# The output gate moved from the weights of a 1024x1024 projection to the product in PSUM, by column halves

## The chip, the cores and the metric

The kernel runs on one core of one Trainium2 chip. The metric is device time in microseconds, and the time of before is 2444.82 us, the median of three runs from 2443.37 to 2444.92 us.

The engines are written as in the profile. PE is the matrix engine, and PEld is its weight load. DVE is the vector engine, ACT the scalar engine and POOL the third elementwise engine. SP is the queue from which DMA transfers are issued. SBUF is the memory that the engines work in, PSUM the memory that PE writes its products to, and DRAM the memory outside the core.

## The reference

One layer of a transformer-like block runs over 2048 tokens of 1024 channels, in fp32. What the change touches is the line in the middle:

```python
ada = jnp.einsum('bd,lde->lbe', jax.nn.silu(c), w_ada) + b_ada
sh1, sc1, g1, sh2, sc2, g2 = (m[:, None, :] for m in jnp.split(ada[l], 6, axis=-1))
...
h = modulate(rmsnorm(x, norm_mix[l]), sh1, sc1)
o, _, _ = token_mixers(h @ w_in[l], lb_f, lb_b, first, hf_c, hb_c, *mix_args)
x = x + g1 * (o @ w_out[l])
h2 = modulate(rmsnorm(x, norm_ffn[l]), sh2, sc2)
x = x + g2 * conv_ffn(h2, w_up[l], conv_w[l], conv_b[l], w_down[l], rows)
...
return rmsnorm(x, norm_final)
```

`g1` is one row of 1024 numbers that comes from the conditioning vector `c`. It multiplies the columns of the product `o @ w_out`. Multiplying the columns of `w_out` by it beforehand gives the same product.

## The kernel before, in words

**Products.** Every large product is made in three fp32r matmuls: each operand is split into a rounded high part and a low part that holds the rest, and high x high, high x low and low x high are added up in PSUM. A split is a cast on ACT (L133) and a subtraction on DVE or POOL (L134).

**Stages.** The first stage, from 0 to about 977 us, makes the input projection and the token mixers. Tasks written as Python generators run beside it: at each slot between groups of products the next piece of a task is emitted when the planner's running count of PE time has passed the number that the task yielded. One of these tasks is `w_out_ops` (L982-997). For each of 8 blocks of 128 rows and for each half of 512 columns it loads the weights, loads the gate broadcast over 128 partitions, multiplies the one by the other on DVE (L993), splits the result, and stores high and low part to the DRAM tensor `wo_d`.

**The out-projection** (the loop over 16 tiles of 128 tokens at the end of the listing) runs from about 978 to 1169 us. The mixers' output of a tile, `o`, comes from DRAM, is cast on ACT and split on DVE one tile ahead. A tile of two PSUM banks, `pd` (called `dn` in the profile, two buffers), takes the products: for each of two halves of 512 columns, eight blocks of three matmuls, so 48 matmuls a tile. Then one addition on DVE adds the residual `x` (L1358, written to `cv`), the sum is stored, and ACT squares it and sums the squares (L1360).

**The second norm.** After every second tile (an odd one) `second_norm` makes the inverse root on POOL (L126, L128), scales both tiles on DVE (L1279), and then, spread over the products of the next two tiles by the yielded waits, transposes them on PE into the PSUM tiles `ux` and `uz` (L69), applies scale and shift on ACT (L1292) and makes the combinations and splits that the next stage reads (L1295 and on). "Even transition" below is what stands between an odd tile's second half and the second half of the even tile after it; "odd transition" is the other one.

**The order.** Instructions are not issued in the order of the source: a scheduler lays each engine's list out when the kernel is built, and each engine then runs its list strictly in order, with waits on the others. The later stages are up-products with the convolution (to about 2008 us) and the down-product with the last norm.

Of the kernel before, what the change touches and what calls it, by code (L numbers as in the profile page):

```python
# [9 lines left out]
F32 = mybir.dt.float32  # L10
F32R = mybir.dt.float32r
# [7 lines left out]
P = 128  # L19
D = 1024  # L20
# [13 lines left out]
AL = 512  # L34
# [14 lines left out]
def view(t, off, dims):  # L49

    return bass.AP(t.tensor, t.offset + off, [list(t.ap[0])] + [list(d) for d in dims])
# [32 lines left out]
def tile_trunk(ctx, tc, x, c, cx, c_ctx, w_ada, b_ada, norm_mix, norm_ffn, w_in, hg_norm, sgu_g, sgu_b,  # L84
               w_sp, b_sp, w_out, w_up, conv_w, conv_b, w_down, norm_final, masks, out):
    nc = tc.nc
    V, S, G, T = nc.vector, nc.scalar, nc.gpsimd, Tensor(nc.tensor)
    ld = nc.sync.dma_start
    st = nc.sync.dma_start
# [3 lines left out]
    w_ada, w_in, w_out, w_up, w_down = w_ada[0], w_in[0], w_out[0], w_up[0], w_down[0]  # L93
# [21 lines left out]
    g_d = dr.tile([2, D], F32, name="g_d")  # L115
# [3 lines left out]
    wo_d = dr.tile([P, NK, 2, D], F32, name="wo_d")  # L119
# [3 lines left out]
    def rstd(pool, ss, n, scale, bias=EPS, keep=lambda i: i, out=None):  # L123

        r = pool.tile([P, 8], F32, tag="rs", name="rs")
        keep(G.tensor_scalar(out=r[:, :n], in0=ss, scalar1=scale, scalar2=bias, op0=ALU.mult, op1=ALU.add))  # L126
        r2 = pool.tile([P, 8], F32, tag="rs2", name="rs2") if out is None else out
        G.tensor_tensor(out=r2[:, :n], in0=r[:, :n], in1=mhalf[:, :n], op=ALU.pow)  # L128
        return r2

    def split(hi, lo, raw, eng=None, keep=lambda i: i):

        keep(S.copy(hi, raw))  # L133
        (eng or G).tensor_sub(lo, raw, hi.bitcast(F32))  # L134
# [56 lines left out]
    with es1:  # L191
# [22 lines left out]
        def raw_tile():  # L214
            return p1.tile([P, D], F32, tag="raw", name="raw", bufs=3)
# [766 lines left out]
        def w_out_ops():  # L982

            for k in range(NK):
                for n in range(2):
                    cl = slice(n * 512, n * 512 + 512)
                    raw = raw_tile()
                    w, g = raw[:, :512], raw[:, 512:]
                    ld(w, w_out[k * P:(k + 1) * P, cl])
                    ld(g, g_d[0:1, cl].broadcast_to([P, 512]))  # L990
                    yield 5.0
                    hi = pm.tile([P, 512], F32, tag="acc", name="wo_hi")
                    V.tensor_mul(w, w, g)  # L993
                    split(hi.bitcast(F32R), g.bitcast(F32R), w, V)
                    st(wo_d[:, k, 0, cl], hi)
                    st(wo_d[:, k, 1, cl], g)
                    yield 2.5

        def w_down_ops():

# [174 lines left out]
    px = esx.enter_context(tc.tile_pool(name="px", bufs=1, reuse_waits="tile"))  # L1175
# [17 lines left out]
    def dbank():  # L1193
        return ps2.tile([P, 2, 512], F32, tag="dn", name="dn", bufs=2)
# [4 lines left out]
    def v_tile():  # L1199
        return px.tile([P, TH + GW], F32, tag="cv", name="cv", bufs=3)  # L1200

    def c_tile():
        return px.tile([P, NK, P], F32R, tag="fl", name="fl", bufs=2, align_bytes=AL)
# [70 lines left out]
    with tc.tile_pool(name="po", bufs=1, reuse_waits="tile") as po:  # L1274
        def second_norm(hh, g0, xs, ss, bank_, first, step):

            r = rstd(px, ss, 2, 1.0 / D)
            for i in range(2):
                scaled.append(V.tensor_scalar(out=xs[i], in0=xs[i], scalar1=r[:, i:i + 1], scalar2=None, op0=ALU.mult))  # L1279
            yield first  # L1280
            cl = slice(g0 // 2 * P, g0 // 2 * P + P)
            for k in range(4):
                pt = bank_()
                for kk in range(2):
                    for i in range(2):
                        o = kk * 256 + i * P
                        T.transpose(pt[:, o:o + P], xs[i][:, (k + 4 * kk) * P:(k + 4 * kk + 1) * P], ident)
                yf = c_tile()
                fl = yf.bitcast(F32)
                for kk, dims in ((0, [[7 * P, 2], [1, P]]), (1, [[4 * P, 2], [1, P]])):  # L1290
                    kq = k + 4 * kk
                    pin(S.activation(view(fl, kk * P, dims),  # L1292
                                     pt[:, kk * 256:kk * 256 + 256].rearrange("p (i c) -> p i c", c=P),
                                     AF.Identity, bias=s2[:, kq:kq + 1], scale=a2[:, kq:kq + 1]))
                pin(V.tensor_sub(fl[:, 3:5, :], view(fl, 7 * P, [[-2 * P, 2], [1, P]]), view(fl, 0, [[7 * P, 2], [1, P]])))  # L1295
                V.tensor_sub(fl[:, 2, :], fl[:, 5, :], fl[:, 3, :])
                V.tensor_sub(fl[:, 6, :], fl[:, 1, :], fl[:, 2, :])
                hi = px.tile([P, 7, P], F32R, tag="yst", name="yst", bufs=2, align_bytes=AL)
                a = b = 0
                if hh == 0:  # L1300
                    a, b = NR, NR - 1
                    S.copy(xah[:, :, k, cl], fl[:, :a, :])
                    V.tensor_sub(xal[:, :, k, cl], fl[:, :b, :], xah[:, :b, k, cl].bitcast(F32))
                    V.tensor_sub(yf[:, b:a, :], fl[:, b:a, :], xah[:, b:a, k, cl].bitcast(F32))
                split(hi[:, a:, :], yf[:, a:7, :], fl[:, a:7, :], V)
                st(yd[hh][:, 0, a:, k, cl], hi[:, a:, :].bitcast(F32))
                st(yd[hh][:, 1, b:, k, cl], fl[:, b:7, :])
                yield step

        tiles = [(0, g) for g in range(NCH)] + [(1, g) for g in range(NCH)]  # L1310

        nt_ = len(tiles)

        def fetch_o(t):
            hh, g = tiles[t]
            raw = raw_tile2(2 * (t % 2 == 0)).rearrange("p a b -> p (a b)").rearrange("p (k c) -> p k c", c=P)
            ld(raw, oT_d[hh][:, :, g * P:(g + 1) * P])
            return raw

        def split_o(t, raw):  # L1320
            o = po.tile([P, 2, NK, P], F32R, tag="o", name="o", align_bytes=AL) if t % 2 else first_o[0]()
            split(o[:, 0], o[:, 1], raw, V, pin)
            return o

        def fetch_x(t):
            xt = raw_tile2(2 if t == nt_ - 1 else 1 + 2 * (t % 2))
            ld(xt.rearrange("p a b -> p (a b)"), x[t * P:(t + 1) * P, :])
            return xt.rearrange("p a b -> p (a b)")

        raw_o = {1: fetch_o(1)}  # L1330
        xts = {0: fetch_x(0)}
        ops = {0: first_o[1]}
        xs = []
        for t, (hh, g) in enumerate(tiles):
            if g % 2 == 0:
                ss = px.tile([P, 2], F32, tag="ss", name="ss", bufs=2)
            if t + 2 < nt_:
                raw_o[t + 2] = fetch_o(t + 2)
            if t + 1 < nt_:
                ops[t + 1] = split_o(t + 1, raw_o.pop(t + 1))  # L1340
                xts[t + 1] = fetch_x(t + 1)
            if t + 2 == nt_:
                units[0].load()
            if t + 1 == nt_:
                units[1].load_half(0)
            pd = dbank()
            o = ops.pop(t)
            for n in range(2):
                for k in range(NK):
                    mm3(pd[:, n, :], o[:, 0, k, :], o[:, 1, k, :], wo[k][:, 0, n * 512:(n + 1) * 512],  # L1350
                        wo[k][:, 1, n * 512:(n + 1) * 512], k == 0, k == NK - 1)
                    if t + 1 < nt_ or n == 0 and k < 4:
                        bg_q.slot()
            if t + 1 == nt_:
                for n in range(3):
                    prep(n)
            xn = v_tile()[:, :D]
            V.tensor_add(xn, pd.rearrange("p a b -> p (a b)"), xts.pop(t))  # L1358
            st(xn_d[t], xn)
            S.activation(pd.rearrange("p a b -> p (a b)"), xn, AF.Square, accum_out=ss[:, g % 2:g % 2 + 1])  # L1360
            if t + 1 == nt_:
                units[1].load_half(1)
            xs.append(xn)
            if g % 2:
                how = (ubank, 6.0, 3.0) if t + 1 < nt_ else (lambda: dbank()[:, 0, :], 9.0, 4.5)
                norm = second_norm(hh, g - 1, xs, ss, *how)
                if t + 1 < nt_:
                    bg_q.drain()
                wait = next(norm)
                bg_q.drain()  # L1370
                bg_q.add(norm)
                bg_q.at = T.t + wait
                xs = []
# [193 lines left out]
    for n, (u, i) in enumerate(prods):  # L1567
# [10 lines left out]
        p = zbank() if i == 1 else u.z if i in (4, 6) else u.x  # L1578
        hi, lo = u.A[i]
# [40 lines left out]
    V = Kept(nc.vector, pin)  # L1620
# [111 lines left out]
    xts, odd_ss = {}, {}  # L1732
# [131 lines left out]
```

## Time and profile before

| what | value |
|---|---|
| median of three runs | 2444.82 us |
| the profiled execution, its own time | 2441.35 us |
| its span in the trace | 2439.6 us |
| mean granted clock of PE | 0.997 of full |
| PE busy | 2403.6 us, 99% of the span |
| DVE busy | 1669.5 us, 68% |
| ACT busy | 1039.4 us, 43% |
| POOL busy | 882.7 us, 36% |

The profiled execution's own time is 1.75 us more than its span, and it is 3.47 us (0.14%) below the median of the three runs. In the rows of a timeline the first number is the start, the second the length; "x48" joins 48 instructions of one kind, and the bracket tells how long the engine sat idle and what ended it. A PE matmul's length contains its way through the array, so that rows of consecutive matmuls overlap. In a table of windows each engine has its busy time in a stretch of the span, and behind it the granted clock, the DMA share and the GB/s.

### The profile page before, as it was taken

Reading aid. Unit: us, or ns where it says so; the run is one execution under the profiler, and the core shown is the slowest. Engines: PE = TensorE matmul, PEld = TensorE weight load, DVE = VectorE, ACT = ScalarE, POOL = GpSimd, SP = SyncE. Lnnn points to the kernel's source line nnn. Section 1 sums busy time; section 2 is a strip of 40 time slices with the busy share of each in tenths; the row PEclk is TensorE's granted clock in tenths of the full one; section 3 lists DMA queues with packets and bytes.
Section 4 is the critical chain, followed back from the end, with each engine's and each line's share of the span. In section 5 each row is a group of like instructions: output and inputs, shape, how many; then the busy total and the mean of one; then the engine's idle time right before and its main releaser. Section 6 shows DMA issues by size and latency. Waiting matters only on the chain.

```text
span 2439.6 us, 32382 instructions
## 1 busy us (share of the span) xinstructions
PE 2403.6 (99%) x11711; PEld 1995.0 (82%) x11711; DVE 1669.5 (68%) x2293; ACT 1039.4 (43%) x1802; POOL 882.7 (36%) x796
## 2 busy tenths in 40 slices
PE   8999999999999999999999999999999999999998
PEld 5887887888888887788888888888888887888887
DVE  5867795756776786465596666639866772776875
ACT  4554334434444443354554444434445442332343
POOL 1232110110121132000688778787888870000002
PEclk9999999999999999999999999999999999999999
DMA  8365446573354323768922322562222238934745
GB/s 311 108 209 163 152 136 196 193 241 121 113 177 156 104 104 141 239 209 260 309 82 86 97 81 91 183 230 97 86 94 86 88 112 334 324 121 147 229 153 196
DMA packets 307853, 400.10 MB, mean 164 GB/s; under 512 B 33113, under 2 KB 216161, under 8 KB 304621
## 3 DMA queue, kind: packets, MB, share of 16 engines
q1 hardware_dynamic: 304404, 397.28, 48.3%
q8 instruction: 92, 1.51, 0.2%
q10 hardware_dynamic: 3289, 0.76, 0.1%
q14 instruction: 68, 0.56, 0.1%
HBM read 288.85 MB, written 109.13 MB: 163 GB/s over the span
## 4 chain that ended last, share of the span: by engine, by line
PE 47%; issue 2%; POOL 1%; DVE 1%; ACT 1%; SPq 0%; DMA 0%; POOLq 0%; ACTq 0%
PE ux L65 19%; PE uz L65 14%; PE dn L65 14%; POOL ra L1723 0%; POOL rr L1724 0%; DVE dn L1434 0%; POOL Al L134 0%; ACT mhl L133 0%; ACT jk L1715 0%; DVE odd L80 0%; ACT odd L1793 0%; DVE mhl L80 0%; DVE thl L80 0%; ACT thl L133 0%; POOL raw L1243 0%
## 5 line engine op out<-in xcount | busy, mean ns | idle before, releaser
L1434 DVE SCALAR_TENSOR_TENSOR dn<-gp,taps,dn 128x1024 f32<-128x1024 f32 x352 | 448.3, 1285 | 97.2 <-ACT dn L1431 92.8
L65 PE MATMUL dn<-thl,mhl 128*128 128x512 f32 x1680 | 381.5, 389 | 1.2 <-ACT thl L133 1.2
L65 PEld LDWEIGHTS dn<-thl,mhl 128*128 128x128 f32 x1680 | 315.1, 188 | 67.6 <-ACT thl L133 2.1
L134 POOL TENSOR_TENSOR Al<-raw,Ah 128x512 fp32r<-128x512 f32 x264 | 341.3, 1309 | 69.3 <-ACT Ah L133 40.5
L65 PE MATMUL pj<-xh,whi 128*128 128x512 f32 x896 | 362.4, 405 | 0.0
L65 PE MATMUL pj<-xl,whi 128*128 128x512 f32 x896 | 351.3, 392 | 0.6 <-POOL xl L134 0.6
L65 PE MATMUL pj<-xh,wlo 128*128 128x512 f32 x896 | 350.9, 392 | 0.9 <-DVE wlo L134 0.9
L133 ACT CAST Ah<-raw 128x512 fp32r<-128x512 f32 x264 | 163.0, 620 | 240.4 <-PE ux L65 134.6
L65 PE MATMUL ux<-xah,Ah 128*128 128x512 f32 x528 | 205.7, 390 | 0.3 <-ACT keep L1498 0.3
L65 PEld LDWEIGHTS pj<-xh,wlo 128*128 128x128 f32 x896 | 168.4, 188 | 36.9 <-DVE wlo L134 1.1
L65 PEld LDWEIGHTS pj<-xh,whi 128*128 128x128 f32 x896 | 168.9, 189 | 33.7 <-issue 3.5
L65 PEld LDWEIGHTS pj<-xl,whi 128*128 128x128 f32 x896 | 169.1, 189 | 31.9 <-POOL xl L134 1.5
L65 PE MATMUL dn<-wo,o 128*128 128x512 f32 x768 | 182.9, 394 | 1.7 <-DVE nt L717 0.9
L65 PE MATMUL uz<-yf,Ah 128*128 128x512 f32 x704 | 174.0, 389 | 0.0
L590 POOL TENSOR_TENSOR K<-K,tot 128x512 f32<-128x512 f32 x40 | 58.3, 1458 | 303.8 <-DVE tot L520 158.0
L65 PEld LDWEIGHTS dn<-wo,o 128*128 128x128 f32 x768 | 142.0, 188 | 31.6 <-issue 1.1
L65 PE MATMUL ux<-yf,Ah 128*128 128x512 f32 x528 | 155.4, 389 | 0.0
L65 PEld LDWEIGHTS uz<-yf,Ah 128*128 128x128 f32 x704 | 132.1, 188 | 27.4
L65 PE MATMUL ux<-xah,Al 128*128 128x512 f32 x528 | 141.7, 390 | 1.0 <-POOL Al L134 1.0
L65 PE MATMUL ux<-xal,Ah 128*128 128x512 f32 x352 | 137.1, 389 | 0.0
L1723 POOL TENSOR_SCALAR ra<-ss 128x1 f32<-128x1 f32 x8 | 5.3, 662 | 360.4 <-ACT jk L1715 360.4
L134 DVE TENSOR_TENSOR wlo<-raw,whi 128x1024 fp32r<-128x1024 f32 x68 | 85.1, 1252 | 72.6 <-ACT whi L133 70.7
(345 smaller groups left out, 4480.5 us busy)
## 6 DMA issues: line engine op xcount, KB each, us to landing
raw<-in_w_up_dram SPq DMA_DIRECT2D x88, 512.0 KB
mr<-m SPq DMA_DIRECT2D x85, 512.0 KB
raw<-in_w_in_dram SPq DMA_DIRECT2D x68, 512.0 KB
sT<-wd SPq DMA_DIRECT2D x88, 256.0 KB
raw<-in_w_ada_dram SPq DMA_DIRECT2D x32, 512.0 KB
yf<-yd SPq DMA_DIRECT2D x14, 1024.0 KB
m<-cv SPq DMA_DIRECT2D x22, 544.0 KB
raw<-in_w_down_dram SPq DMA_DIRECT2D x22, 512.0 KB
```

The costliest lines, as they stand in the source:

```text
L65: return self.engine.matmul(out, lhsT, rhs, **kw)
L133: keep(S.copy(hi, raw))
L134: (eng or G).tensor_sub(lo, raw, hi.bitcast(F32))
L590: e.tensor_mul(view(K2, row * W + o, src), view(K, o, src), view(tot, t0, [[4, n], [ts, 2], [0, B]]))
L1434: V.scalar_tensor_tensor(out=cr, in0=gt[:, t // 3:t // 3 + RH, t % 3:t % 3 + GW], scalar=taps[:, t * NF + f:t * NF + f + 1], in1=cr, op0=A ...
L1723: G.tensor_scalar(out=a, in0=ss, scalar1=plus, scalar2=None, op0=ALU.add)
```

## The change

`w_out_ops` no longer reads the gate. It loads whole rows of 1024 columns, splits the two column halves without a multiplication, and stores the low part in one transfer of 512 KB instead of two of 256 KB. Where it was 16 pieces of two loads each, it is 8 pieces with one load, and the yielded waits are 9.0 behind the load, 4.0 between the halves and 2.5 at the end, where they were 5.0 and 2.5 for each half.

In the out-projection two tiles of 128x512 are filled once with the broadcast gate, by two DMAs that are issued behind the loads of `o` for tile 1 and of `x` for tile 0. For each half a multiplication on DVE gates the product in place in PSUM (L1354) and an addition on DVE adds the residual (L1355), so four DVE instructions of 512 columns stand where one addition of 1024 stood. In the source the first pair stands between the two halves' products. The first yielded wait of `second_norm` goes from 6.0 to 6.5, and for the last one from 9.0 to 10.0.

```diff
--- before.py
+++ after.py
@@ -982,19 +982,18 @@
         def w_out_ops():
 
             for k in range(NK):
+                raw = raw_tile()
+                ld(raw, w_out[k * P:(k + 1) * P, :])
+                yield 9.0
                 for n in range(2):
                     cl = slice(n * 512, n * 512 + 512)
-                    raw = raw_tile()
-                    w, g = raw[:, :512], raw[:, 512:]
-                    ld(w, w_out[k * P:(k + 1) * P, cl])
-                    ld(g, g_d[0:1, cl].broadcast_to([P, 512]))
-                    yield 5.0
                     hi = pm.tile([P, 512], F32, tag="acc", name="wo_hi")
-                    V.tensor_mul(w, w, g)
-                    split(hi.bitcast(F32R), g.bitcast(F32R), w, V)
+                    split(hi.bitcast(F32R), raw[:, cl].bitcast(F32R), raw[:, cl], V)
                     st(wo_d[:, k, 0, cl], hi)
-                    st(wo_d[:, k, 1, cl], g)
-                    yield 2.5
+                    if n == 0:
+                        yield 4.0
+                st(wo_d[:, k, 1, :], raw)
+                yield 2.5
 
         def w_down_ops():
 
@@ -1329,6 +1328,10 @@
 
         raw_o = {1: fetch_o(1)}
         xts = {0: fetch_x(0)}
+        gate = []
+        for n, w in enumerate(("Ah", "Al")):
+            gate.append(px.tile([P, 512], F32, tag=w, name=f"gate{n}", bufs=4, align_bytes=AL))
+            ld(gate[n], g_d[0:1, n * 512:n * 512 + 512].broadcast_to([P, 512]))
         ops = {0: first_o[1]}
         xs = []
         for t, (hh, g) in enumerate(tiles):
@@ -1345,24 +1348,31 @@
                 units[1].load_half(0)
             pd = dbank()
             o = ops.pop(t)
+
+            def gated(n):
+                sl = slice(n * 512, n * 512 + 512)
+                V.tensor_mul(pd[:, n, :], pd[:, n, :], gate[n])
+                V.tensor_add(xn[:, sl], pd[:, n, :], xt[:, sl])
             for n in range(2):
                 for k in range(NK):
                     mm3(pd[:, n, :], o[:, 0, k, :], o[:, 1, k, :], wo[k][:, 0, n * 512:(n + 1) * 512],
                         wo[k][:, 1, n * 512:(n + 1) * 512], k == 0, k == NK - 1)
                     if t + 1 < nt_ or n == 0 and k < 4:
                         bg_q.slot()
+                if n == 0:
+                    xn, xt = v_tile()[:, :D], xts.pop(t)
+                    gated(0)
             if t + 1 == nt_:
                 for n in range(3):
                     prep(n)
-            xn = v_tile()[:, :D]
-            V.tensor_add(xn, pd.rearrange("p a b -> p (a b)"), xts.pop(t))
+            gated(1)
             st(xn_d[t], xn)
             S.activation(pd.rearrange("p a b -> p (a b)"), xn, AF.Square, accum_out=ss[:, g % 2:g % 2 + 1])
             if t + 1 == nt_:
                 units[1].load_half(1)
             xs.append(xn)
             if g % 2:
-                how = (ubank, 6.0, 3.0) if t + 1 < nt_ else (lambda: dbank()[:, 0, :], 9.0, 4.5)
+                how = (ubank, 6.5, 3.0) if t + 1 < nt_ else (lambda: dbank()[:, 0, :], 10.0, 4.5)
                 norm = second_norm(hh, g - 1, xs, ss, *how)
                 if t + 1 < nt_:
                     bg_q.drain()
```

Three places show what the scheduler makes of it. The first is PE's list at the start of the out-projection: `dn` is the PSUM tile, and `wo` with or without a number is a tile of two or of one row block of the weights. Before, behind the last block of tile 0's first half comes its second half, without a wait on DVE:

```order
L65 MATMUL dn<-wo_8311,o 128x512 [waits DMAHW1_49]
L65 MATMUL dn<-wo_8311,o 128x512 x2
L65 MATMUL dn<-wo,o 128x512 x9
L65 MATMUL dn<-wo_8307,o 128x512 [waits DMAHW2_49]
L65 MATMUL dn<-wo_8307,o 128x512 x2
L65 MATMUL dn<-wo_8308,o 128x512 [waits DMAHW3_49]
L65 MATMUL dn<-wo_8308,o 128x512 x2
L65 MATMUL dn<-wo_8309,o 128x512 [waits DMAHW4_49]
```

In the changed kernel the same place reads so, from the last block of tile 0's first half on:

```order
L65 MATMUL dn<-wo_8255,o 128x512 [waits DMAHW1_49]
L65 MATMUL dn<-wo_8255,o 128x512 x2
L65 MATMUL dn<-wo,o 128x512 [waits Activation_49]
L65 MATMUL dn<-wo,o 128x512
L65 MATMUL dn<-wo,o 128x512 [waits DVE_49]
L65 MATMUL dn<-wo,o 128x512 x3
L65 MATMUL dn<-wo,o 128x512 [waits DVE_49]
L65 MATMUL dn<-wo,o 128x512 x8
L65 MATMUL dn<-wo_8251,o 128x512 [waits DMAHW2_49]
L65 MATMUL dn<-wo_8251,o 128x512 x2
```

Six matmuls now stand between the halves; they belong to tile 1's first half, and they wait for ACT's cast and for DVE's subtraction of tile 1's `o`. The matmul behind them, with the third wait in this piece, is the first of tile 0's second half. The semaphore value that it waits for is the one that DVE reaches with the addition to the first half of the same `dn` tile (L1355).

The second place is PE's list in an even transition, the one from tile 3 to tile 4. Before, from the last block of tile 3's second half through tile 4's first half (its first matmul waits for ACT, its third for DVE's subtraction) into tile 4's second half:

```order
L65 MATMUL dn<-wo_8311,o 128x512 x3
L65 MATMUL dn<-wo,o 128x512 [waits PE_49,Activation_49]
L65 MATMUL dn<-wo,o 128x512
L65 MATMUL dn<-wo,o 128x512 [waits DVE_49]
L65 MATMUL dn<-wo,o 128x512 x6
L65 MATMUL dn<-wo_8307,o 128x512 x3
L65 MATMUL dn<-wo_8308,o 128x512 x3
L65 MATMUL dn<-wo_8309,o 128x512 x3
L65 MATMUL dn<-wo_8310,o 128x512 x3
L65 MATMUL dn<-wo_8311,o 128x512 x3
L65 MATMUL dn<-wo,o 128x512 x3
L69 MATMUL ux<-ident,cv 128x128 [waits DVE_49] x2
```

Now, from the point at which 14 matmuls have finished tile 4's first half:

```order
L65 MATMUL dn<-wo,o 128x512 [waits DVE_49,Activation_49]
L69 MATMUL ux<-ident,cv 128x128 [waits DVE_49,PE_49]
L69 MATMUL uz<-ident,cv 128x128 [waits PE_49]
L65 MATMUL dn<-wo,o 128x512
L69 MATMUL ux<-ident,cv 128x128 [waits PE_49]
L69 MATMUL uz<-ident,cv 128x128 [waits PE_49]
L65 MATMUL dn<-wo,o 128x512 [waits DVE_49]
L65 MATMUL dn<-wo,o 128x512 x2
L69 MATMUL ux<-ident,cv 128x128 [waits DVE_49]
L69 MATMUL ux<-ident,cv 128x128 x2
L69 MATMUL uz<-ident,cv 128x128 x3
L65 MATMUL dn<-wo,o 128x512 [waits DVE_49]
```

Behind tile 4's first half stand five matmuls of tile 5 and ten transposes, with waits on ACT's cast of the next `o`, on DVE's scaled tiles and on DVE's subtraction. The last row is the first matmul of tile 4's second half, which waits for DVE's addition to the first half. Before, tile 4's second half followed its first directly, without a wait, and the first transposes lay in that second half.

The third place is DVE's list at the same transition. Before, one addition (L1358), then the two scalings of the norm with the subtraction for the next `o` between them:

```order
L1358 TENSOR_TENSOR cv<-dn,raw 128x1024 [waits DMAHW2_49,PE_49]
L1279 TENSOR_SCALAR cv<-cv,rs_8842 128x1024 [waits DMAHW6_49,Pool_49]
L134 TENSOR_TENSOR o<-raw,o 128x1024 [waits DMAHW3_49,Activation_49]
L1279 TENSOR_SCALAR cv<-cv,rs_8842 128x1024 [waits DMAHW7_49,DVE_49]
L1295 TENSOR_TENSOR fl<-fl 128x256 [waits DMAHW4_49,Activation_49]
```

Now, from the gating of tile 3's second half to the addition of tile 4's first half (L1278 is the scaling, which was L1279; `gate_8460` and `gate_8462` are the two halves of the gate):

```order
L1354 TENSOR_TENSOR dn<-dn,gate_8462 128x512 [waits PE_49]
L1355 TENSOR_TENSOR cv<-dn,raw 128x512 [waits DVE_49]
L1278 TENSOR_SCALAR cv<-cv,rs_8802 128x1024 [waits DMAHW2_49,Pool_49]
L1354 TENSOR_TENSOR dn<-dn,gate_8460 128x512 [waits PE_49]
L134 TENSOR_TENSOR o<-raw,o 128x1024 [waits DMAHW5_49,Activation_49]
L1278 TENSOR_SCALAR cv<-cv,rs_8802 128x1024 [waits DMAHW1_49,DVE_49]
L1355 TENSOR_TENSOR cv<-dn,raw 128x512 [waits DMAHW3_49,DVE_49]
```

The multiplication of tile 4's first half stands behind the first scaling, and its addition behind the subtraction for the next `o` and behind the second scaling. In an odd transition nothing of the norm stands ahead of the pair but the subtraction and the combinations of one block.

## The prediction

> **What bounds the kernel now.** I read the page first, then the windows and the waits of the out-projection, then its timeline at two places.
>
> ```profile
> span 2439.6 us, 32382 instructions
> PE 2403.6 (99%) x11711; PEld 1995.0 (82%) x11711; DVE 1669.5 (68%) x2293; ACT 1039.4 (43%) x1802; POOL 882.7 (36%) x796
> ...
> L65 PE MATMUL dn<-wo,o 128*128 128x512 f32 x768 | 182.9, 394 | 1.7 <-DVE nt L717 0.9
> ```
>
> PE is busy for 99% of the span, so any microsecond in which PE waits longer is a microsecond of time, and work on another engine costs only where PE waits for it. The 768 matmuls of the out-projection have 1.7 us of idle time ahead of them, in all. The windows of that stage say the same of every stretch behind the first 12 us:
>
> ```profile
> 978.00:990.00 12.00, 11.76 (x50) 9.14 (x50) 0.72 (x1) 1.05 (x1) 1.22 (x1) 1.00 1.07 382
> 990.00:1010.00 20.00, 19.47 (x88) 15.94 (x88) 7.50 (x10) 5.28 (x9) 0.89 (x2) 1.00 0.57 190
> 1010.00:1070.00 60.00, 60.00 (x285) 49.12 (x284) 38.08 (x79) 32.38 (x59) 1.78 (x4) 1.00 0.67 209
> 1070.00:1168.00 98.00, 97.47 (x455) 79.59 (x455) 58.41 (x99) 47.37 (x77) 8.91 (x12) 1.00 0.79 250
> ```
>
> The columns are PE, PEld, DVE, ACT, POOL, then clock, DMA share and GB/s. PE is full from 1010 to 1070 us, while DVE is busy for 38.08 of 60 us. The waits of the stage, complete, are four:
>
> ```profile
> PE dn L65 <- DVE nt L717: 0.9, 1, 0.9
> PE ux L69 <- DVE cv L1279: 0.5, 1, 0.5
> PE dn L65 <- DVE o L134: 0.5, 1, 0.5
> PE dn L65 <- ACT o L133: 0.2, 1, 0.2
> ```
>
> None of them is between the two halves of a tile. The change puts one there, in all 16 tiles: the second half's first matmul waits for DVE's addition to the first half, because both halves lie in one PSUM tile. So the pair "beside the second's products" stands ahead of them. What decides is what PE has to do in the meantime, and how late DVE is.
>
> **Durations of the new operations.** The trace has the same shapes in the up-products:
>
> ```profile
> L1513 DVE TENSOR_TENSOR uz<-uz,keep x22: 691/693/700, 1224.1 to 1987.6; 128x512 f32<-128x512 f32 x22
> L1515 DVE TENSOR_TENSOR cv<-uz,cv x22: 681/685/691, 1225.9 to 1989.4; 128x512 f32<-128x512 f32 x22
> L1358 DVE TENSOR_TENSOR cv<-dn,raw x16: 1218/1221/1225, 990.4 to 1169.1; 128x1024 f32<-128x1024 f32 x16
> ```
>
> A multiplication of 128x512 in place in PSUM takes 0.693 us, and one from PSUM to SBUF takes 0.685. A tile's end then costs DVE 2 x (0.693 + 0.685) = 2.76 us where the addition took 1.22, so 16 tiles cost 16 x 1.54 = 25 us more of DVE. DVE had over a third of the stage free; only what lies in the chain to a second half counts.
>
> **Term 1: the start.**
>
> ```profile
> 977.94 11.12 PE L65 MATMUL dn<-wo,o 128*128 128x512 f32 x48 [0.94 <-DVE nt L717]
> 979.67 0.57 SPq L1317 DMA_DIRECT2D raw<-oT  x1
> 980.29 2.65 SPq L1327 DMA_DIRECT2D raw<-in_x_dram  x1
> 983.03 0.53 SPq L1317 DMA_DIRECT2D raw<-oT  x1
> ...
> 988.21 1.05 ACT L133 CAST o<-raw 128x1024 fp32r<-128x1024 f32 x1 [11.46 <-DMA raw<-oT]
> 989.28 1.23 DVE L134 TENSOR_TENSOR o<-raw,o 128x1024 fp32r<-128x1024 f32 x1 [11.49 <-ACT o L133]
> 989.30 0.30 PEld L65 LDWEIGHTS dn<-wo,o 128*128 128x128 f32 x2 [0.66 <-ACT o L133]
> 989.30 0.73 PE L65 MATMUL dn<-wo,o 128*128 128x512 f32 x2 [0.24 <-ACT o L133]
> ...
> 990.56 1.66 PE L65 MATMUL dn<-wo,o 128*128 128x512 f32 x6 [0.53 <-DVE o L134]
> ```
>
> Before, tile 0's 48 matmuls ran from 977.94 to 989.06, 11.12 / 48 = about 0.23 us each, and this hid the load of tile 1's `o`, which ACT could cast only from 988.21. Now only the first half runs, to about 983.5. The next six matmuls need tile 1's `o`: two can go at 989.30, four at 990.56. DVE then has the gate's multiplication behind the subtraction that begins at 989.28: 990.43 to 991.12, and the addition to 991.8. Tile 0's second half starts there. At 990.56 before, 50 matmuls were done; now at 991.8 there are 30 done, and the 20 missing take 20 x 0.227 = 4.5 us, to 996.3. The loss is 5.8 us, **taken as 6**. It holds if the gate's first half, whose DMA is issued on SP behind `x` for tile 0 (about 983.0) and pushes tile 2's `o` back by two issues, has landed by 990.4. The stretch moves 382 GB/s at a full DMA share, and `o` of tile 1 took from 979.67 to 988.21, 8.5 us. With the same 8.5 us a gate issued at 983.0 lands at 991.5, 1 us late; if it lands at once nothing is added. The bounds are 4.5 (the 20 matmuls alone) and 9.
>
> After such an idle stretch PE's clock may fall. The trace has one example:
>
> ```profile
> 412.00:416.00 4.00, 1.30 (x5) 0.52 (x3) 2.97 (x5) 2.16 (x3) 0.00 (x0) 0.98 0.62 188
> 416.00:420.00 4.00, 3.92 (x11) 3.11 (x12) 4.00 (x6) 1.54 (x3) 0.00 (x0) 0.59 0.34 131
> ```
>
> Idle for 2.7 of 4 us was followed by 4 us at a granted clock of 0.59, which loses 0.41 x 4 = 1.6 us. The idle here is longer, and I add **1.5** (0 to 3). The Trainium skill, "TensorE: Matmul & The Clock Gate", "Part 1: The HAM clock gate", says that one idle window of about 3.4 us takes the clock to half until about 3.4 us of work have passed. By that rule the sum would have half of 3.4, 1.7 us, an estimate; the row agrees in kind, though its idle time was in two pieces.
>
> **Term 2: even transitions.** T is the end of an odd tile's second half. The chain can be read off before's transition, whose rows give the distances:
>
> ```profile
> 1025.18 1.22 DVE L1358 TENSOR_TENSOR cv<-dn,raw 128x1024 f32<-128x1024 f32 x1 [0.35 <-PE dn L65]
> ...
> 1049.06 1.23 DVE L1358 TENSOR_TENSOR cv<-dn,raw 128x1024 f32<-128x1024 f32 x1 [0.57 <-PE dn L65]
> ...
> 1050.32 1.03 ACT L1360 ACTIVATE dn<-cv 128x1024 f32<-128x1024 f32 x1 [2.68 <-DVE cv L1358]
> ...
> 1051.38 1.03 ACT L133 CAST o<-raw 128x1024 fp32r<-128x1024 f32 x1
> ...
> 1052.64 0.75 DVE L1279 TENSOR_SCALAR cv<-cv,rs 128x1024 f32<-128x1024 f32 x1 [2.35 <-POOL rs L128]
> 1053.31 1.22 DVE L134 TENSOR_TENSOR o<-raw,o 128x1024 fp32r<-128x1024 f32 x1
> 1054.44 0.75 DVE L1279 TENSOR_SCALAR cv<-cv,rs 128x1024 f32<-128x1024 f32 x1
> ...
> 1059.07 0.60 PE L69 MATMUL uz<-ident,cv 128*128 128x128 f32 x4
> 1059.40 0.77 PEld L65 LDWEIGHTS dn<-wo,o 128*128 128x128 f32 x4
> 1059.42 0.95 PE L65 MATMUL dn<-wo,o 128*128 128x512 f32 x3
> ```
>
> With 0.2 us from PE to DVE (an estimate; 0.05 is what PE took behind DVE, from 990.51 to 990.56): gate and add to T+1.6, square from T+1.63, first scaling 2.32 us later (1050.32 to 1052.64) at T+3.95, then the even tile's multiplication 0.67 later at T+4.62, the subtraction for the next `o` at T+5.31, the second scaling 1.13 later at T+6.44, the addition from T+7.11 to T+7.8. The even tile's second half starts at **T+7.85**.
>
> What PE has until then: 14 matmuls of the first half, 5 of the next tile and 10 transposes (4 take 1059.42 - 1059.07 = 0.35 us, so 0.9 to 1.1 for 10). That is 19 x 0.227 + 1.0 = 5.3 us. So PE idles 2.4 to 2.6 us, mostly in waits for ACT's cast, DVE's scaling and DVE's subtraction. The odd transition has 29 matmuls and 6 transposes, about 7.1 us, and DVE there has no norm ahead of the pair, so PE does not wait. A pair of tiles then takes 23.9 + 2.4 = 26.3 us, where before it took 1049.06 - 1025.18 = 23.9. Seven even transitions inside the stage: 7 x 2.4 = **17 us**. If DVE and ACT hand over faster than I took, a pair loses 1.8 (12.6 in all); if the chain has a further operation of 0.4 us in it, 2.8 (20). Tile 1's transition, where nothing of the norm is due but tile 2's `o` is, costs about **0.6** (0 to 1.5). The last tile has seven up-products to cover its chain: 0.
>
> **Term 3: the weights' task.** It loses 16 multiplications and 16 loads of 256 KB.
>
> ```profile
> L993 DVE TENSOR_TENSOR raw<-raw x16: 664/692/694, 373.6 to 500.6; 128x512 f32<-128x512 f32 x16
> ...
>   DMA raw<-g_d: 29.8, 12
> ```
>
> That takes 16 x 0.692 = 11 us from DVE, and 29.8 us in which DVE stood idle ahead of them for the gate's broadcast. In the stretch around, from 360 to 520 us, PE waits for only this:
>
> ```profile
> PE mi L69 <- DVE nt L709: 1.6, 1, 1.6
> PE sc L65 <- ACT kh L798: 1.5, 1, 1.5
> PE sc L65 <- DVE kl L800: 1.3, 1, 1.3
> ```
>
> These 4.4 us, with the 1.6 us of clock that the 412-416 stretch cost, are the most that the task's relief can give: -6. DVE's order around them changes little, and a wait that was moved can as well land in another place, +3. I take **0**.
>
> **Sum.** 6 + 1.5 + 17 + 0.6 + 0 = 25 us on the profiled execution's 2441.35 gives 2466.4; on the median of the three runs, 0.14% above it, it gives 2469.8. I name 2468, 1.0% slower.
>
> **Rivals.**
>
> *The idle pieces cost clock as well, in every even transition.* Idle of 2.8 us in two waits was enough at 412. In an even transition 2.5 us come in three waits of about 0.8, with work between. If each is followed by the loss of the row above, 1.6 us, then 7 x 1.6 = 11 us more: 2479. If the slow stretch also delays the odd tile's first half it stays inside that figure, since DVE is not late there. Against it: 4 us of window there held 1.30 us of matmuls, while here 7.85 us hold 5.3. The Trainium skill, in the same page under "A second HAM failure mode: psum-queue depth-cycling", says that frequent short idle between groups of matmuls makes the clock swing between half and full; no row of before shows it, and this rival is what it would do here.
>
> *The fill covers the wait, and the task's relief pays.* The point from which it decides is T+5.3: if the addition to an even tile's first half is done by then, PE never stands. That needs the chain 2.5 us shorter, which could be if the POOL step ends earlier or if the multiplication is not held by the scaling. Then only the start remains, 6 to 7.5 us, less up to 6 from the task: 2441 to 2445, the same as before or slightly faster. Against it stands DVE's strict order: the multiplication is behind the first scaling, which is behind POOL, which is behind the square of the tile that ended at T.
>
> *The start is worse.* If the gate or `x` lands late under the full DMA share, every microsecond goes straight into tile 0's second half: 5 us late gives 2473.
>
> **Chances.** My forecast with its bounds, 2455 to 2475, gets 62%. The clock rival, 2475 to 2490, gets 20%, the late gate another 5%, inside the same range. The covered wait gets 8%, of which half is faster. The remaining 5% are for a smaller loss than my lower bound, 2446 to 2455. The range from 2451 to 2488 leaves out the covered wait and the far tails. A measurement of this kernel can tell about 0.2%, 5 us, from no change: faster than that gets 4%, within it 6%, slower 90%.
>
> **What would show it.** In the changed profile the waits of this stage should name DVE's L1355 ahead of `dn`, with the largest single wait near 983 to 989 us for ACT's cast of `o`; PE's windows in the stage should be full in odd transitions and miss about 2.5 us in each even one; the addition at DVE should end 7.8 us behind the end of the odd tile's matmuls; the clock should fall behind 983 and nowhere else. If PE's windows are full from 1010 to 1070, term 2 is wrong. If the time between two even tiles' second halves is 26 us and the clock stays at 1.0, terms and mechanism are right.

## The result, and the profile after

The changed kernel takes 2472.10 us (median of four runs, 2471.62 to 2473.58) against 2444.87 us for the one before: a ratio of 1.0119 with a 95% interval from 1.0107 to 1.0131, 27.2 us slower. The prediction was 2468. Two executions among those below, one of the kernel before (5123 us) and the profiled one of the kernel with tile 0 exempt (3443 us, at a granted clock of 0.654), are far slower than their like and are left out of every figure, so that tile 0 exempt is judged by its times alone.

The page of the changed kernel, its first two lines and the group of the out-projection's matmuls:

```profile
span 2470.1 us, 32397 instructions
PE 2412.8 (98%) x11711; PEld 1996.7 (81%) x11711; DVE 1680.2 (68%) x2325; ACT 1039.0 (42%) x1802; POOL 882.8 (36%) x796
...
L65 PE MATMUL dn<-wo,o 128*128 128x512 f32 x768 | 192.2, 402 | 17.6 <-ACT o L133 10.2
```

The same matmuls now have 17.6 us of idle time ahead of them, where they had 1.7. All waits of PE from 975 to 1205 us:

```profile
PE dn L65 <- ACT o L133: 10.2, 8, 6.7
PE dn L65 <- DVE o L134: 7.2, 13, 0.8
PE ux L69 <- DVE cv L1278: 3.9, 7, 0.6
PE dn L65 <- DVE cv L1355: 0.2, 1, 0.2
```

The addition L1355, for which the second halves wait, is charged with only 0.2 us. This is how a wait looks when the order is already bent around it: the time is lost one step earlier, at the matmuls that stand between the halves, and these wait for ACT's cast, DVE's subtraction and DVE's scaling.

**The start.** The out-projection begins earlier than before (its first matmul was at 977.9 us):

```profile
L65 PE MATMUL dn<-wo,o x768: 387/389/796, 972.7 to 1195.2; 128*128 128x512 f32 x192
```

Its timeline behind the first half of tile 0, and the windows there (columns as before, the clock is the third from the end):

```profile
975.64 0.59 SPq L1316 DMA_DIRECT2D raw<-oT  x1
976.28 2.73 SPq L1326 DMA_DIRECT2D raw<-in_x_dram  x1
979.06 0.90 SPq L1334 DMA_DIRECT2D gate<-g_d  x2
...
984.02 1.04 ACT L133 CAST o<-raw 128x1024 fp32r<-128x1024 f32 x1 [11.30 <-DMA raw<-in_x_dram]
985.09 1.23 DVE L134 TENSOR_TENSOR o<-raw,o 128x1024 fp32r<-128x1024 f32 x1 [11.34 <-ACT o L133]
...
985.11 14.38 PE L65 MATMUL dn<-wo,o 128*128 128x512 f32 x50 [6.68 <-ACT o L133]
986.24 0.69 DVE L1354 TENSOR_TENSOR dn<-dn,gate 128x512 f32<-128x512 f32 x1
...
986.96 0.69 DVE L1355 TENSOR_TENSOR cv<-dn,raw 128x512 f32<-128x512 f32 x1
```

```profile
982.00:984.00 2.00, 0.00 (x0) 0.00 (x0) 0.00 (x0) 0.00 (x0) 0.00 (x0) 0.92 1.04 394
984.00:986.00 2.00, 0.89 (x2) 0.50 (x2) 0.91 (x1) 1.04 (x1) 0.00 (x0) 0.50 1.12 345
986.00:988.00 2.00, 1.96 (x5) 1.34 (x5) 1.62 (x3) 0.00 (x0) 0.00 (x0) 0.50 0.79 278
988.00:990.00 2.00, 2.00 (x7) 1.52 (x6) 0.00 (x0) 0.00 (x0) 0.00 (x0) 0.50 0.84 251
990.00:992.00 2.00, 2.00 (x9) 1.64 (x8) 0.00 (x0) 0.00 (x0) 0.00 (x0) 0.87 0.02 4
```

PE stands for 6.7 us, and then works at a granted clock of 0.50 until 990: 5 matmuls in 2 us, then 7, where 9 fit into the next window, at 0.87. The gate is not late: its multiplication follows the subtraction directly (986.24). The bracket of ACT's cast names the load of `x`, which was issued behind that of `o`; at the same place in the kernel with two PSUM tiles, further down, it names `raw<-oT`, the load of `o`.

**An even transition**, with the operations in the order that the prediction gave them. The odd tile's last gating begins at 1060.50:

```profile
1060.50 0.70 DVE L1354 TENSOR_TENSOR dn<-dn,gate 128x512 f32<-128x512 f32 x1 [1.50 <-PE dn L65]
...
1061.96 1.03 ACT L1370 ACTIVATE dn<-cv 128x1024 f32<-128x1024 f32 x1 [3.81 <-DVE cv L1355]
1063.02 1.03 ACT L133 CAST o<-raw 128x1024 fp32r<-128x1024 f32 x1
...
1064.10 0.50 PE L65 MATMUL dn<-wo,o 128*128 128x512 f32 x1 [0.47 <-ACT o L133]
1064.28 0.75 DVE L1278 TENSOR_SCALAR cv<-cv,rs 128x1024 f32<-128x1024 f32 x1 [2.35 <-POOL rs L128]
1064.95 0.69 DVE L1354 TENSOR_TENSOR dn<-dn,gate 128x512 f32<-128x512 f32 x1
1065.18 0.30 PE L69 MATMUL ux<-ident,cv 128*128 128x128 f32 x1 [0.58 <-DVE cv L1278]
...
1066.82 0.98 PE L65 MATMUL dn<-wo,o 128*128 128x512 f32 x3 [0.77 <-DVE o L134]
1067.35 0.68 DVE L1355 TENSOR_TENSOR cv<-dn,raw 128x512 f32<-128x512 f32 x1
...
1068.21 7.08 PE L65 MATMUL dn<-wo,o 128*128 128x512 f32 x30
```

The three idle brackets of PE, 0.47, 0.58 and 0.77 us, are the larger part of the loss. The even tile's addition ends at 1068.03. With the odd tile's matmuls ending about 0.2 us before its gating (the prediction's estimate), at 1060.3, that is 7.7 us, and the prediction had 7.8. In the odd transition behind it PE has one wait, of 0.21 us:

```profile
1078.68 0.71 PE L65 MATMUL dn<-wo,o 128*128 128x512 f32 x2
1079.60 10.74 PE L65 MATMUL dn<-wo,o 128*128 128x512 f32 x46 [0.21 <-DVE o L134]
```

### The profile page after: what moved, and what is told of

It reads as the page before. It is cut to its first block, busy times and chain, and to the rows that moved or that the text cites. A ratio compares the mean times of both kernels' runs of the same rounds, so it can differ in the third digit from the quotient of the medians.

```text
span 2470.1 us, 32397 instructions
## 1 busy us (share of the span) xinstructions
PE 2412.8 (98%) x11711; PEld 1996.7 (81%) x11711; DVE 1680.2 (68%) x2325; ACT 1039.0 (42%) x1802; POOL 882.8 (36%) x796
## 4 chain that ended last, share of the span: by engine, by line
PE 46%; issue 2%; POOL 1%; DMA 1%; DVE 1%; ACT 1%; SPq 0%; POOLq 0%; ACTq 0%; DVEq 0%
PE ux L65 19%; PE uz L65 14%; PE dn L65 13%; POOL ra L1733 0%; DMA mr<-m 0%; DMA sT<-wd 0%; POOL rr L1734 0%; DMA raw<-in_w_up_dram 0%; POOL Al L134 0%; ACT mhl L133 0%; POOL fl L1238 0%; DVE dn L1444 0%; ACT jk L1725 0%; DVE odd L80 0%; ACT odd L1803 0%
## 5 line engine op out<-in xcount | busy, mean ns | idle before, releaser
L65 PE MATMUL dn<-wo,o 128*128 128x512 f32 x768 | 192.2, 402 | 17.6 <-ACT o L133 10.2
```

What stands on the lines that cost most here:

```text
L65: return self.engine.matmul(out, lhsT, rhs, **kw)
```

## The experiments

Each is the changed kernel or the kernel before with one edit. The expectations speak of theory W: that the loss is the wait of a second half for the addition to the first. The runs came in three groups, and in each the kernel before was measured again, with medians of 2443.67, 2444.85 and 2442.86 us; each ratio is to that. The changed kernel was measured only beside the 2444.87 above, so a difference from it is uncertain by up to 2 us.

**Both gatings behind all products.**

```diff
                 if n == 0:
                     xn, xt = v_tile()[:, :D], xts.pop(t)
-                    gated(0)
...
+            gated(0)
             gated(1)
```

> The changed kernel with both gatings issued behind the second half's products, so that no second half waits for an addition; DVE has the same four instructions a tile. Theory W (the loss is the wait of a second half's first matmul for the addition to the first half): the out-projection goes back from 222 us to 190 to 193 us, PE's waits there are below 4 us in all, and the time is 2438 to 2444 us, since the 5 us that the first stage gained stay. Rival D (the loss is DVE's 25 us of further work, wherever it stands): DVE is as busy as in the changed kernel, so at least 2462 us.

Measured: 2454.78 us, 1.0043 of the kernel before (1.0028 to 1.0058). Rival D's bound is missed, and so is W's. 17.3 us of the loss went with the wait; about 10 stayed. PE's three largest waits from 970 to 1200 us:

```profile
PE ux L69 <- DVE cv L1278: 5.3, 8, 1.2
PE dn L69 <- DVE cv L1278: 3.2, 2, 1.8
PE dn L65 <- ACT o L133: 1.7, 1, 1.7
```

No second half waits any more. What waits is the norm's transposes, for the scaling. At a tile's end DVE has four operations, where it had one, ahead of the square, and the scaling comes that much later. So there is a second cost that the wait between the halves does not explain. A further part of what stayed belongs to the down-product, see "The layout kept".

**A PSUM tile for each half.**

```diff
-            pd = dbank()
+            ph = [dbank(), dbank()]
...
-                V.tensor_mul(pd[:, n, :], pd[:, n, :], gate[n])
-                V.tensor_add(xn[:, sl], pd[:, n, :], xt[:, sl])
+                V.tensor_mul(ph[n][:, 0, :], ph[n][:, 0, :], gate[n])
+                V.tensor_add(xn[:, sl], ph[n][:, 0, :], xt[:, sl])
```

> The changed kernel with each half's product in a PSUM tile of its own, so that the first half's gating can run beside the second half's products, as the change says. Theory W: no wait between the halves, 2437 to 2443 us, within 2 us of the kernel with both gatings behind the products. Rival D (DVE's further work): at least 2462 us. Rival P (DVE working in PSUM beside PE's writes slows either): DVE's 128x512 multiplications above 0.75 us, or PE's matmul spacing above 0.23 us, and 2446 us or more.

Measured: 2446.54 us, 1.0009 (1.0000 to 1.0019): 25.6 us less than the changed kernel, with the same four DVE operations a tile. Rival D falls. W's range up to 2443 us is missed as well, by less than what the layout costs (see "The layout kept"). It is 8 us better than both gatings behind the products, not within 2 us, because now only the second pair stands in the chain. DVE's operations take 0.69 us as before, and from 1020 to 1098 us PE is full, so rival P falls too. Its own waits above 0.5 us are two: 3.6 us at the start and 1.9 us for the norm's scaling.

**How much a pair of tiles takes** is read from POOL's step of the norm, once a pair, at the same place in each kernel: before, changed, both behind, two PSUM tiles.

```profile
1028.02 0.70 POOL L128 TENSOR_TENSOR rs<-rs,mhalf 128x2 f32<-128x2 f32 x1
1051.91 0.70 POOL L128 TENSOR_TENSOR rs<-rs,mhalf 128x2 f32<-128x2 f32 x1
```

```profile
1036.86 0.70 POOL L128 TENSOR_TENSOR rs<-rs,mhalf 128x2 f32<-128x2 f32 x1
1063.55 0.70 POOL L128 TENSOR_TENSOR rs<-rs,mhalf 128x2 f32<-128x2 f32 x1
```

```profile
1027.05 0.70 POOL L128 TENSOR_TENSOR rs<-rs,mhalf 128x2 f32<-128x2 f32 x1
1051.73 0.69 POOL L128 TENSOR_TENSOR rs<-rs,mhalf 128x2 f32<-128x2 f32 x1
```

```profile
1026.92 0.70 POOL L128 TENSOR_TENSOR rs<-rs,mhalf 128x2 f32<-128x2 f32 x1
1050.72 0.69 POOL L128 TENSOR_TENSOR rs<-rs,mhalf 128x2 f32<-128x2 f32 x1
```

That is 23.9, 26.7, 24.7 and 23.8 us. Of the 2.8 us that the change adds to a pair, 2.0 go with the wait between the halves, and the other 0.8 with the longer chain behind the tile. With a tile for each half both go, as far as these pairs show.

**The weights' part alone.** The new `w_out_ops` in the kernel before, with the out-projection of before, so that the gate is left out of the computation.

> The kernel before with the new task for the weights alone; the out-projection is that of before, and the gate is left out of the computation. Theory W with its account (the first stage gains 5 us by the task's relief): the out-projection starts at 972 to 974 us instead of 977.9, and the time is 2438 to 2441 us. Rival S (the first stage's gain is lost again at the down-product's start, where the changed kernel's profile shows PE waiting 3 us longer): 2443 to 2446 us.

Measured: 2437.94 us, 0.9973 (0.9963 to 0.9983), 5.7 us faster than the kernel before. The first out-projection matmul is at 972.0 us. Rival S falls: PE waits 1.2 us at the down-product's start, as before.

**Tile 0 exempt.**

```diff
-                    gated(0)
+                    if t:
+                        gated(0)
...
+            if t == 0:
+                gated(0)
             gated(1)
```

> The changed kernel with tile 0 alone gated behind both halves. Theory W: the idle of 6.7 us ahead of tile 1's products and the drop of the clock behind it go, 2461 to 2465 us, 7 to 11 less than the changed kernel. Rival O (the start is bound by the load of tile 1's output from the mixers, which PE waits for in any order): 2469 to 2472 us, and the clock falls all the same.

Measured: 2461.18 us (median of four), 10.9 us less than the changed kernel, or 9.7 when each is taken against the kernel before of its own group, as W has it. Rival O falls by the time. That the idle time and the drop of the clock went, as W says, no profile shows.

**Even tiles exempt, and odd tiles exempt.** The same edit with `t % 2 == 0 and t` and with `t % 2` in place of `t == 0`.

> The changed kernel with the even tiles from 2 on gated behind both halves; tile 0 and the odd tiles as changed. Theory W (the seven even transitions carry the larger part of the loss, 2.8 us each): 17 to 21 us less than the changed kernel, less what the longer chain of such a tile to the products behind it costs, so 2451 to 2458 us, with PE waiting in the stage only at the start and behind the norm's scaling. Rival E (each transition pays alike, the odd ones too): 2461 to 2464 us.

> The changed kernel with the odd tiles gated behind both halves; the even ones as changed. If only even transitions pay (the prediction's account): no gain, and up to 1.4 us more a pair since an odd tile's end now has the longer chain to the norm's scaling, 2472 to 2482 us, and a pair takes 26.7 to 28.1 us. If odd transitions pay as well (the even exempt kernel's pair took 25.5 us where one without any wait between halves took 24.7): a pair takes 25.8 to 26.5 us and the time is 2464 to 2471 us.

Measured: 2464.34 us with the even tiles exempt and 2464.95 with the odd ones, 7.8 and 7.2 us less than the changed kernel; against the kernel before of its own group the second is 5.1. The even exempt case missed W's range and came out 0.3 us above the rival's, "each transition pays alike". In the profiled execution its seven pairs together took 11.1 us less than the changed kernel's (179.94 against 191.03), but everything behind them took 3.7 us more, for a reason that no run isolates. POOL's step starts at 1035.49 and 1060.99 us with the even tiles exempt, and at 1061.28 and 1087.24 with the odd ones.

A pair takes 25.5 and 26.0 us (one of the six pairs with the odd tiles exempt took 26.9). From 26.7, exempting the even tiles gives 1.2 back, exempting the odd ones 0.7, and exempting both gave 2.0: the two add up. Each exemption also changes what the scheduler puts between the other tiles' halves, so the split by parity holds for these orders, not for the changed kernel alone.

**The layout kept.** In the changed kernel's profile the down-product also loses time, with no edit near it. The matmuls that read `thl`, and the tail, before and changed:

```profile
L65 PE MATMUL dn<-thl,mhl x1680: 388/389/504, 2028.6 to 2410.1; 128*128 128x512 f32 x187
L65 PE MATMUL dn<-thl,tail x24: 388/389/389, 2412.4 to 2431.9; 128*128 128x512 f32 x24
```

```profile
L65 PE MATMUL dn<-thl,mhl x1680: 387/389/504, 2054.8 to 2440.8; 128*128 128x512 f32 x187
L65 PE MATMUL dn<-thl,tail x24: 388/389/389, 2443.1 to 2462.6; 128*128 128x512 f32 x24
```

From the first of them to the tail it took 383.8 us, and now 388.3. One of SP's waits there names the cause, and the timeline shows what ends it:

```profile
SPq L1662 <- PE dn L65: 11.5, 1, 11.5
```

```profile
2054.57 0.39 PE L65 MATMUL dn<-Ah,mhl 128*128 128x512 f32 x1
2054.99 0.32 SPq L1662 DMA_DIRECT2D sS<-m  x1
```

The gate's two tiles borrow the tags `Ah` and `Al` and are the first to be allocated under them. The reading behind the edit is that a tag's address is given by its first allocation, so that these tags move into the memory that the down-product's first load of `sS` takes over. No view shows the addresses. That load now waits for the last matmul that reads `Ah`, which by the rows is one of the down-product's own first blocks (not an up-product, as the expectation below has it), and the loads behind it on SP wait with it. The edit puts empty allocations of the other tags ahead:

```diff
+        for n in range(2):
+            px.tile([P, 2], F32, tag="ss", name="ss", bufs=2)
+            raw_tile2(2 + n)
+        for n in range(3):
+            v_tile()
...
         gate = []
```

> The changed kernel with empty allocations ahead of the gate's two tiles, so that the tiles behind them lie where they lay before; no engine's work is changed. Theory L (the gate's tiles, allocated first, move the upper operands' tiles into memory that the down-product's first load takes over, and the load then waits for the last up-product's matmul): that wait of 11.5 us on SP and PE's 3.7 us of waits at the down-product's start go, the stage from its first matmul to its tail's takes 384 us instead of 388, and the time is 2466 to 2469 us. Rival M (the later start comes from the memory traffic of that moment): 2471 to 2473 us.

> The kernel with a PSUM tile for each half, and with the layout kept. Theory L: 4 to 6 us less than the same kernel without the layout, 2440 to 2443 us, within 4 us of the kernel before. Rival M: 2445 to 2448 us.

Measured: 2467.87 us for the changed kernel with it, 4.2 less; 2441.73 for the one with two PSUM tiles, 4.8 less, and 0.9989 of the kernel before (0.9980 to 0.9999). Theory L holds in both, since only allocations were added: the wait of 11.5 us is in neither trace, and the down-product takes 383.8 us from 2055.4 to 2439.2 in the first and 383.9 in the second.

**What the weights' task gains by.** Three kernels on the base of before. One keeps the multiplications without the gate's loads (it squares the weights and leaves the gate out):

```diff
                     hi = pm.tile([P, 512], F32, tag="acc", name="wo_hi")
+                    V.tensor_mul(raw[:, cl], raw[:, cl], raw[:, cl])
```

> The kernel before with the new weights' task, in which each half is multiplied by itself on DVE, so that the 16 multiplications stay and only the gate's 16 loads and the waits for them go; the gate is left out of the computation and the weights are squared. If the first stage's gain comes from DVE standing in its queue behind those loads: as the weights' part alone, 2436 to 2440 us. If it comes from the 11 us of multiplications: 2442 to 2446 us.

Measured: 2436.41 us, 0.9969 (0.9958 to 0.9981). DVE's 11 us of multiplications were not the cost. The next changes the distance alone:

```diff
-                    yield 5.0
+                    yield 7.5
...
-                    yield 2.5
+                    yield 0.0
```

> The kernel before, with the gate still in the weights and every load still there; only the distance that the weights' task yields behind its loads is 7.5 instead of 5.0, and 0 instead of 2.5 behind its stores. Theory Q (the first stage's gain comes from DVE no longer standing in its queue for a load that has not landed): most of the 29.8 us of DVE's idle time ahead of the multiplications goes, and the time is 2436 to 2441 us. Rival B (it comes from the 4 MB less of loads): DVE's idle time may go, and the time stays at 2443 to 2446 us.

Measured: 2444.84 us, 1.0005 (0.9996 to 1.0014), no change. It doesn't decide between its theories, since the wait that it was to remove stayed:

```profile
DVE raw L993 <- DMA raw<-g_d: 29.7, 10, 6.8
```

The last loads whole rows and the gate's whole row beside each, and multiplies the gate into the weights:

```diff
                 ld(raw, w_out[k * P:(k + 1) * P, :])
+                gt = raw_tile()
+                ld(gt, g_d[0:1, :].broadcast_to([P, D]))
                 yield 9.0
+                V.tensor_mul(raw, raw, gt)
```

> The kernel before, with the new task by whole rows at its distance of 9.0, but with the gate still loaded, one row of 1024 for each block, and multiplied into the weights. Theory Q: 2436 to 2441 us, as the change of distance alone. Rival B (the loads' bytes): 2443 to 2446 us.

Measured: 2440.23 us, 0.9991 (0.9983 to 1.0000). That is in theory Q's range, but it is only 2.6 us below the kernel before of its own group, with 13.7 us of DVE's wait left for `raw<-g_d`. Less waiting and less time go together through these (29.8 and 29.7 us of wait with no gain, 13.7 with 2.6, none for the gate with 5.7 and 8.4). But the bytes went with the waits in the two fastest, so that whether DVE's place in its queue or the 4 MB of loads is the cause stays open.

**The gate first.** The kernel with two PSUM tiles and the layout kept, with tile 0's `x` and the gate loaded ahead of tile 1's `o`, and tile 0's gating ahead of tile 1's split.

> The kernel with a PSUM tile for each half and the layout kept, with the gate and x of tile 0 loaded ahead of tile 1's output of the mixers, and with tile 0's gating ahead of tile 1's split on DVE. If the 3.8 us that PE waits for tile 0's addition come from DVE's order (the gating stood behind the split, which stood behind its load): the wait is below 2.5 us, the clock does not fall behind it, and the time is 2437 to 2440 us. If the load of tile 1's output is what PE waits for in any order: the wait bears ACT's or DVE's o instead and is as long, 2440 to 2444 us.

Measured: 2442.21 us, 0.9997 (0.9988 to 1.0006). PE's largest wait is now named after ACT's cast of `o`, and it has grown from 3.8 to 5.5 us:

```profile
PE dn L65 <- ACT o L133: 5.5, 1, 5.5
```

The time and the wait are those of the second theory. But that the load of tile 1's `o` is what PE waits for in any order is not shown. ACT had waited for tile 0's addition, and its cast stands directly behind tile 0's square:

```profile
984.45 1.03 ACT L1386 ACTIVATE dn<-cv 128x1024 f32<-128x1024 f32 x1 [14.53 <-DVE cv L1369]
985.50 1.97 ACT L133 CAST o<-raw 128x1024 fp32r<-128x1024 f32 x2
```

So the order on ACT may hold the cast as well as the load. What the run shows is that this order gains nothing.

## Why the prediction came out right, point by point

**What bounds the kernel**: right. The time was lost where PE waited, and DVE's 25 us of added work is not what costs: with a PSUM tile for each half and the layout kept the same work costs about 3 us (the kernel is 3.1 us faster than before, the weights' part alone 5.7), and PE's wait at the start is 3.8 us there.

**The sum** by terms, each against the run that isolates it:

| term | predicted | measured | from |
|---|---|---|---|
| start, with the clock | 7.5 | 9.7 | tile 0 exempt |
| even transitions | 17 | 19.9 | seven pairs, odd transitions included: 191.03 - 171.18 |
| tile 1 | 0.6 | not isolated | |
| the weights' task | 0 | -5.7 | the weights' part alone |
| the down-product's start | not seen | 4.2 | the layout kept |
| sum | 25 | 28.1 | measured in all: 27.2 |

The total was 2 us off by luck: the start, the pairs and the down-product cost 2.2, 2.9 and 4.2 us more than predicted, and the gain of 5.7 us that was taken as 0 made up for more than half of that.

The two profiled executions give the same account without other runs. Their stretches are cut at the first matmul of the out-projection and at POOL's first and last step of the norm (L128):

| stretch | before | changed | difference |
|---|---|---|---|
| to the first matmul | 977.94 | 972.73 | -5.21 |
| start and tile 1, to POOL's step at 1004.10 and at 1010.21 | 26.16 | 37.48 | 11.32 |
| seven pairs, to POOL's step at 1175.28 and at 1201.24 | 171.18 | 191.03 | 19.85 |
| everything behind | 1264.32 | 1268.86 | 4.54 |
| span | 2439.6 | 2470.1 | 30.5 |

That is 3.3 us more than 27.2, because the profiled execution of before was 3.5 us below its median and that of the changed kernel 0.2 below.

**Start.** The mechanism was right: tile 1's `o` sets when PE goes on, and the gate's two transfers were in time. Under-sized were two things. The first stage ended 5.2 us earlier, and `o` was ready only 4.2 us earlier (984.02 against 988.21), so PE stood 6.7 us, where the working had 5.8 (983.5 to 989.3). And the clock cost more: it was at 0.50 from 984 to 990 and at 0.87 in the next 2 us, while PE was at work from 985.1, so about 2.7 us, not 1.5. The Trainium skill's rule ("TensorE: Matmul & The Clock Gate", "Part 1: The HAM clock gate") has the clock fall after an idle window of about 3.4 us, and it does, behind 6.7 us. The prediction's estimate by that page, 1.7 us, was too low here; PE worked without a break (it was busy for 1.96 of the 2 us from 986), and why the return took 5 us of work is not shown.

**Transitions.** The chain was read rightly to within 0.2 us, and so were the three things that PE waits for. Their sum was read too high, 2.4 to 2.6 us for 1.8. A pair's extra 2.8 us are 2.0 idle (24.66 us busy in the 26.69 from 1036.86 to 1063.55, where before PE was busy throughout) and about 0.8 that the profile counts as busy: a matmul that is followed by a wait takes up to 0.50 us (1064.10), where in a row one begins every 0.23. The prediction left this out. It also took the odd transitions to be free ("so PE does not wait"); exempting the odd tiles gives back 0.7 us a pair. One of its signs did not come: the waits name L1355 with only 0.2 us, and the working itself had put the idle time elsewhere.

**The weights' task.** The step that failed is "I take 0". The waits named there did go: from 360 to 520 us PE waits 0.5 us in the changed kernel, where it waited 4.4. The bound of -6 held what was measured, and the choice within it was wrong.

**The clock rival** happened in part. One of the changed kernel's pairs, and four windows of the same kernel with the layout kept, ran at a granted clock of 0.94, although the prediction had the clock fall at the start "and nowhere else"; such a pair took 27.7 to 28.7 us instead of 26.7 to 27.0. The Trainium skill's rule on short idle times (same page, "A second HAM failure mode: psum-queue depth-cycling") is seen here, but not in every transition.

```profile
1090.00:1117.00 27.00, 24.97 (x114) 19.43 (x112) 17.50 (x36) 12.51 (x23) 1.11 (x4) 1.00 0.59 190
1117.00:1146.00 29.00, 26.31 (x113) 20.77 (x112) 16.72 (x28) 12.08 (x19) 1.24 (x3) 0.94 0.76 240
```

## What to carry to other kernels

Work "beside" a half needs that half in a tile of its own: where waits are kept by whole tiles, two halves in one PSUM tile are one after the other, and the loss shows up not at the wait but at whatever the scheduler puts in between. Before a new tile borrows another's tag, ask what the first allocation does to the addresses behind it, since a load a thousand microseconds later can come to wait for another reader. And when two parts of a change are measured together, measure each alone: here a gain of nearly 6 us was buried under a loss of 33.

## What was not expected of the hardware

After 6.7 us of idle the clock stood at 0.50 for 6 us, of which PE worked 5. With the same three waits of 0.5 to 0.8 us in 8 us, some pairs ran at 0.94 and others of the same kernel at 1.00, so these waits alone do not settle whether the clock drops. DVE working in one PSUM tile beside PE's writes to another showed no slowdown on either side: 0.69 us for 128x512, and PE busy for all 78 us from 1020 to 1098.
